# State-space mixer of a hybrid block: per-group VectorE products merged, and a subtraction moved to ScalarE biases

## The chip, the cores and the metric

One core of one Trainium2 chip runs the whole program. The metric is the device time of one execution in microseconds, the median of several runs; a profile is taken of one more execution.

## The reference

Two layers over 1024 latent tokens and 256 context tokens, width 1024. Each layer projects the normed tokens into three groups of heads: attention, a bidirectional state-space mixer (SSD) and a long convolution (Hyena, here by trigonometric matrices). Their outputs are concatenated and projected, and an MLP follows. All of it is fp32. The change touches the state-space mixer alone. For each chunk of 128 tokens, with 6 heads in 2 groups of 3:

```python
cum = jnp.cumsum(dtc * a, axis=2)
seg = cum[:, :, :, None, :] - cum[:, :, None, :, :]
decay = jnp.where(tri, jnp.exp(jnp.where(tri, seg, 0.0)), 0.0)
scores = jnp.einsum('bcihn,bcjhn->bcijh', cc, bc) * decay
y_diag = jnp.einsum('bcijh,bcjhp->bcihp', scores * dtc[:, :, None, :, :], xc)
y_off = jnp.einsum('bcihn,bchpn->bcihp', cc, prev) * jnp.exp(cum)[..., None]
```

This is done once forward and once backward in time. B and C (`bc`, `cc`) are shared by the 3 heads of a group.

## The kernel before

The program goes through each layer in three stages: the input projections with their convolutions (`stage_a`), the three mixers beside each other (`stage_b`), then the output projection and the MLP (`out_proj`, `mlp`). Products with weights are done as three fp32r matmuls on split high and low parts (L177, L178, L180; L191 to L193).

`stage_b` merges generators: attention (48 query tiles: scores L191 to L193, row maximum on VectorE L935, exponential on ScalarE L936, reciprocal L937, its spreading by matmul L941 and copy L943, transposes L952 that are copied out by L957 on ScalarE and L955 on VectorE, product with the values L964, L965), the state-space chunks (`ssm`), the convolution's filters and spectra (L1145 to L1181) and in layer 0 the modulation's columns (L307 to L315). The merge sets only the order in which the program is written. The tile framework then schedules: by its own model of the engines' times it decides the order of the instructions on every engine, and each engine runs its own queue strictly in that order, waiting on semaphores. So a change of a few instructions can reorder others that it doesn't touch.

Inside `ssm`, the function `scores(c)` prepares chunk c, for both directions at once. It loads the column sums as rows, broadcast over the partitions (`crow`, 12 x 128; its halves are Q and E, forward and backward), B (`bd`), C (`cd`) and the values (`xb`). A matmul gives B times C per group (L664), VectorE masks it with the two triangles into `gm` (L666), ScalarE takes exponentials of the sums into CE (L668, L669). VectorE subtracts the backward sums of each token from E (L670, one operation of 128 x 768) and takes the smaller of that and the forward difference, head by head (L672, six of 128 x 128); ScalarE takes the exponential (L673). VectorE then forms the masked scores Q and E from it (L678: 2 directions x 2 groups, 128 x 384 each), the values times the step sizes (L681), and the decayed queries CE times C (L683: 2 groups). `outputs(c)` multiplies (L693), adds the skip (L695), gates (L696) and squares (L697); `scaled(c)` finishes the norm (L704 to L715). There are 10 chunks in layer 0, from about 440 to 655 us, and 8 in layer 1, from about 2440 to 2615 us. `crow` alternates between two buffers, CE too. In layer 0, after the mixers, `out_proj` loads the mixers' outputs back (L974) and splits them (L160, L162); beside it the modulation of layer 1 loads its weights (L348) through one buffer that VectorE reads (L353, L355).

Of the kernel before, what the change touches and what calls it, by code (L numbers as in the profile page):

```python
# [12 lines left out]
AF = mybir.ActivationFunctionType  # L13
# [30 lines left out]
def V(t, off, shape):  # L44

    n = int(np.prod(shape))
    v = t[:, off:off + n]
    if len(shape) == 1:
        return v
    if len(shape) == 2:  # L50
        return v.rearrange("p (a b) -> p a b", a=shape[0])
    if len(shape) == 3:
        return v.rearrange("p (a b c) -> p a b c", a=shape[0], b=shape[1])
    return v.rearrange("p (a b c d) -> p a b c d", a=shape[0], b=shape[1], c=shape[2])
# [56 lines left out]
class K:  # L111
# [441 lines left out]
    def ssm(self, i):  # L553
        nc = self.nc
        sub, mul, add = ALU.subtract, ALU.mult, ALU.add
        st0, st1, st2, la, lb = (self.t(s) for s in ("H8", "U2", "H11", "H9", "H10"))
        P = lambda c: V(st0, 384 * c, [384]) if c < 6 else V(st1, 384 * (c - 6), [384]) if c < 9 else V(st2, 0, [384])
        dt, cum, dec, wl = (V(st2, 384 + 120 * j, [10, 12]) for j in range(4))
        spt = V(lb, 1536, [6, 10, 12])

        x = spt[:, 0]
        nc.vector.tensor_tensor(x, self.dtr, self.row(i, "dtb").unsqueeze(1).to_broadcast([128, 10, 12]), op=add)
        e = spt[:, 1]
# [8 lines left out]
        q = spt[:, 4]  # L572
# [9 lines left out]
        p = self.gs()  # L582
# [27 lines left out]
        for c in (8, 9, 0, 7, 1, 6, 2, 5, 3, 4):  # L610
            xb = xbr([4, 128])
            nc.sync.dma_start(xb, self.xbcD[:, 0:4, col(c):col(c) + 128])
            g = self.gs()
# [9 lines left out]
            g = self.gs()  # L623
# [8 lines left out]
        for q, order in enumerate(((8, 9, 0, 1, 2, 3, 4, 5, 6), (9, 8, 7, 6, 5, 4, 3, 2, 1))):  # L632
            r = slice(64 * q, 64 * q + 64)
            for c in order:
                t = tmr([384])[r, :]
                e = nc.vector
                e.tensor_tensor(z3(t), z3(P(c)[r, :]), dec[r, c, 6 * q:6 * q + 6].unsqueeze(2).to_broadcast([64, 6, 64]), op=mul)
                d = P(to(q, c))[r, :]
                e.tensor_tensor(d, d, t, op=add)
        yield 10  # L640

        tc_, yst = self.t("C2"), self.t("U0")
        ld1, ld2 = VRing((la, 0), (lb, 0)), VRing((tc_, 0), (tc_, 640))
        cer, ysr, xfr = VRing((st2, 864), (st2, 1632)), VRing((yst, 0), (yst, 384)), VRing((yst, 768), (tc_, 2176))
        gm, sq = V(tc_, 1280, [2, 2, 128]), V(tc_, 1792, [3, 128])

        def scores(c, done):
            ld, ldx = ld1([20, 128]), ld2([5, 128])
            crow, xz, bd, cd, xb = ld[:, 0:12], ld[:, 12:18], ld[0:64, 18:20], ldx[:, 0:2], ldx[:, 2:5].rearrange("p a b -> p (a b)")
            cols = slice(col(c), col(c) + 128)  # L650
            bc = lambda k: self.xbcD[:, k, cols].rearrange("(g p) t -> p g t", g=2)
            nc.sync.dma_start(bd, bc(0))
            nc.sync.dma_start(cd[0:64], bc(7))
            nc.sync.dma_start(crow, self.cumD[c:c + 1].to_broadcast([128, 12, 128]))
            nc.sync.dma_start(cd[64:128], bc(7))
            nc.sync.dma_start(xz, self.xbcD[:, 1:7, cols])
            nc.sync.dma_start(xb, self.xtD[c][:, 0:384])
            CE = cer([6, 128])
            Q, E = crow[:, 0:6], crow[:, 6:12]
            g = self.gs()  # L660
            if done:
                rms(g)
            for gr in range(2):
                nc.tensor.matmul(g[:, 128 * gr:128 * gr + 128], bd[:, gr, :], cd[0:64, gr, :], start=True, stop=True)  # L664
            R = root(g) if done else None
            nc.vector.tensor_tensor(gm, g[:, 0:256].rearrange("p (a b) -> p a b", a=2).unsqueeze(1).to_broadcast([128, 2, 2, 128]),  # L666
                                    self.tri.unsqueeze(2).to_broadcast([128, 2, 2, 128]), op=mul)
            nc.scalar.activation(CE[0:64], crow[0:64, 0:6], AF.Exp)  # L668
            nc.scalar.activation(CE[64:128], crow[64:128, 6:12], AF.Exp)  # L669
            nc.vector.tensor_tensor(E, E, cum[:, c, 6:12].unsqueeze(2).to_broadcast([128, 6, 128]), op=sub)  # L670
            for h in range(6):
                nc.vector.scalar_tensor_tensor(E[:, h, :], Q[:, h, :], cum[:, c, h:h + 1], E[:, h, :], op0=sub, op1=ALU.min)  # L672
            nc.scalar.activation(E, E, AF.Exp)  # L673

            for gr in range(2):
                h = slice(3 * gr, 3 * gr + 3)
                for q, (x, e) in enumerate(((Q, nc.vector), (E, nc.vector))):
                    e.tensor_tensor(x[:, h], E[:, h], gm[:, q, gr:gr + 1, :].to_broadcast([128, 3, 128]), op=mul)  # L678
            xf = xfr([384])
            for q, x in enumerate((xf, xb)):  # L680
                nc.vector.tensor_tensor(z3(x), z3(xb), dt[:, c, 6 * q:6 * q + 6].unsqueeze(2).to_broadcast([128, 6, 64]), op=mul)  # L681
            for gr in range(2):
                nc.vector.tensor_tensor(CE[:, 3 * gr:3 * gr + 3, :], CE[:, 3 * gr:3 * gr + 3, :],  # L683
                                        cd[:, gr, :].unsqueeze(1).to_broadcast([128, 3, 128]), op=mul)
            return R, (c, xz, ((xf, Q), (xb, E), (P(c), CE)))

        def outputs(c, xz, terms):
# [12 lines left out]
        def rms(p):  # L700

            for t in range(3):
                for b in range(4):
                    nc.tensor.matmul(p[32 * b:32 * b + 32, 256:288], self.ssel[:, t, :], sq[:, t, 32 * b:32 * b + 32], start=t == 0, stop=t == 2)  # L704

        def root(p):
            return self.rsq(None, p[:, 256:288], 32, 1.0 / 192)
# [8 lines left out]

        order = list(range(8)) + ([8, 9] if i == 0 else [])
        (_, cur), done = scores(order[0], None), None
        for n in range(len(order)):
            R, nxt = scores(order[n + 1], done) if n + 1 < len(order) else (None, None)  # L720
            if done and R is None:
                g = self.gs()
                rms(g)
                R = root(g)
            out = outputs(*cur)
            if done:
                scaled(*done, R)
            cur, done = nxt, out
            yield 12
        g = self.gs()  # L730
# [1057 lines left out]
```

## Time and profile before

| | us |
|---|---|
| median of 3 runs (lowest, highest) | 3657.69 (3657.3, 3661.86) |
| the profiled execution | 3666.86 |
| its span, first to last instruction | 3665.1 |
| TensorE busy | 3398.1 (93%) |
| VectorE busy | 1957.7 (53%) |
| ScalarE busy | 1255.7 (34%) |

The busy times are sums over the span, and stages differ: the three engines are read per stretch below. TensorE's end times are modelled, so its busy share is not its peak rate.

### The profile page before, as it was taken

Reading aid. Unit: us, or ns where it says so; the run is one execution under the profiler, and the core shown is the slowest. Engines: PE = TensorE matmul, PEld = TensorE weight load, DVE = VectorE, ACT = ScalarE, POOL = GpSimd, SP = SyncE. Lnnn points to the kernel's source line nnn. Section 1 sums busy time; section 2 is a strip of 40 time slices with the busy share of each in tenths; the row PEclk is TensorE's granted clock in tenths of the full one; section 3 lists DMA queues with packets and bytes.
Section 4 is the critical chain, followed back from the end, with each engine's and each line's share of the span. In section 5 each row is a group of like instructions: output and inputs, shape, how many; then the busy total and the mean of one; then the engine's idle time right before and its main releaser. Section 6 shows DMA issues by size and latency. Waiting matters only on the chain.

```text
span 3665.1 us, 51139 instructions
## 1 busy us (share of the span) xinstructions
PE 3398.1 (93%) x20636; PEld 2785.1 (76%) x20636; DVE 1957.7 (53%) x3172; ACT 1255.7 (34%) x2078; POOL 710.7 (19%) x479
## 2 busy tenths in 40 slices
PE   6899888888888999999999989988998999999999
PEld 3788767667767777888888777867787778888887
DVE  6576688667654766423323367679875332222223
ACT  4565444443332211111111256555434322111111
POOL 1000000011131322232322200000011433333332
PEclk9899989999999999999999999999999999999999
DMA  7345767587741223111111224577476311111112
GB/s 252 118 123 165 190 179 221 160 237 219 269 145 47 103 98 104 52 35 41 40 35 41 72 78 138 150 205 216 140 220 202 92 46 46 47 51 47 46 47 74
DMA packets 263042, 439.24 MB, mean 120 GB/s; under 512 B 33316, under 2 KB 172341, under 8 KB 256790
## 3 DMA queue, kind: packets, MB, share of 16 engines
q1 hardware_dynamic: 231654, 333.86, 29.3%
q0 software_dynamic: 31152, 102.12, 9.8%
q8 instruction: 162, 2.65, 0.3%
q14 instruction: 74, 0.61, 0.1%
HBM read 355.43 MB, written 80.47 MB: 119 GB/s over the span
## 4 chain that ended last, share of the span: by engine, by line
PE 68%; DMA 11%; DVE 10%; issue 7%; ACT 2%; POOL 1%; SPq 0%; POOLq 0%; DVEq 0%; ACTq 0%
PE psum L177 16%; PE psum L180 16%; PE psum L178 16%; PE psum L191 4%; PE psum L192 4%; PE psum L193 4%; DVE D L355 3%; DMA U<-in_wmod_dram 3%; PE psum L964 2%; PE psum L952 1%; DMA H<-cumD 1%; DMA H<-kD 1%; DVE st L935 1%; DMA Wp<-in_t_odd_dram 1%; PE psum L833 1%
## 5 line engine op out<-in xcount | busy, mean ns | idle before, releaser
L177 PE MATMUL psum<-H,Wp 128*128 128x512 f32 (+1 forms) x2112 | 788.5, 374 | 19.0 <-ACT H L160 12.6
L178 PE MATMUL psum<-H,Wp 128*128 128x512 f32 (+1 forms) x2112 | 786.7, 373 | 6.8 <-POOL H L162 5.8
L180 PE MATMUL psum<-H,Wp 128*128 128x512 f32 (+1 forms) x2112 | 679.0, 373 | 2.0 <-POOL Wp L162 1.8
L988 DVE SCALAR_TENSOR_TENSOR H<-psum,mod,H 128x1024 f32<-128x1024 f32 (+2 forms) x440 | 409.4, 955 | 463.0 <-PE psum L180 435.7
L162 POOL TENSOR_TENSOR Wp<-Wr,Wp 128x1024 fp32r<-128x1024 f32 x158 | 403.3, 2553 | 1204.8 <-ACT Wp L160 1185.9
L177 PEld LDWEIGHTS psum<-H,Wp 128*128 128x128 f32 x2112 | 399.0, 189 | 94.5 <-ACT H L160 13.1
L178 PEld LDWEIGHTS psum<-H,Wp 128*128 128x128 f32 x2112 | 398.9, 189 | 78.6 <-POOL H L162 7.3
L160 ACT CAST Wp<-Wr 128x1024 fp32r<-128x1024 f32 (+1 forms) x210 | 216.1, 1029 | 707.5 <-PE psum L180 639.3
L177 PE MATMUL psum<-C,Wp 128*128 128x512 f32 (+1 forms) x1200 | 448.8, 374 | 6.9 <-DVE H L988 6.0
L180 PEld LDWEIGHTS psum<-H,Wp 128*128 128x128 f32 x2112 | 397.4, 189 | 75.7 <-issue 4.6
L178 PE MATMUL psum<-C,Wp 128*128 128x512 f32 (+1 forms) x1200 | 447.3, 373 | 0.0
L1007 DVE TENSOR_TENSOR U<-U 128x1280 f32<-128x1280 f32 (+1 forms) x64 | 90.4, 1415 | 592.0 <-ACT U L1006 318.3
L180 PE MATMUL psum<-C,Wp 128*128 128x512 f32 (+1 forms) x1200 | 369.7, 373 | 0.0
L177 PEld LDWEIGHTS psum<-C,Wp 128*128 128x128 f32 x1200 | 226.2, 189 | 59.3 <-DVE H L988 12.1
L180 PEld LDWEIGHTS psum<-C,Wp 128*128 128x128 f32 x1200 | 226.2, 188 | 43.9
L178 PEld LDWEIGHTS psum<-C,Wp 128*128 128x128 f32 x1200 | 226.5, 189 | 42.3
L1006 ACT ACTIVATE U<-psum 128x1024 f32<-128x1024 f32 x64 | 65.6, 1026 | 515.6 <-PE psum L180 510.8
L355 DVE SCALAR_TENSOR_TENSOR D<-U,cpad,D 128x1024 f32<-128x1024 f32 x84 | 144.5, 1758 | 84.5 <-DMA U<-in_wmod_dram 84.4
L162 POOL TENSOR_TENSOR C<-U,C 128x1280 fp32r<-128x1280 f32 (+1 forms) x64 | 173.6, 2713 | 69.2 <-ACT C L160 69.2
L936 ACT ACTIVATE H<-psum,st 128x1280 f32<-128x1280 f32 x96 | 127.6, 1329 | 133.3 <-DVE st L935 130.4
L191 PE MATMUL psum<-H,H 96*128 96x512 f32 (+3 forms) x356 | 143.9, 404 | 21.0 <-ACT C L957 7.1
L191 PE MATMUL psum<-H,Wp 128*128 128x256 f32 (+1 forms) x464 | 144.5, 314 | 18.4 <-ACT H L403 7.0
(410 smaller groups left out, 5494.6 us busy)
## 6 DMA issues: line engine op xcount, KB each, us to landing
Wr<-in_wff_dram SPq DMA_DIRECT2D x128, 512.0 KB, 3.5
Wp<-in_t_odd_dram POOLq DMA_DIRECT2D x32, 1024.0 KB, 7.0
U<-in_wmod_dram SPq DMA_DIRECT2D x48, 512.0 KB, 3.2
C<-in_wmod_dram SPq DMA_DIRECT2D x32, 512.0 KB, 5.5
Wr<-in_wout_dram SPq DMA_DIRECT2D x32, 512.0 KB, 3.6
Wr<-in_win_dram SPq DMA_DIRECT2D x28, 512.0 KB, 3.3
H<-cumD SPq DMA_DIRECT2D x18, 768.0 KB, 4.8
kD<-H SPq DMA_DIRECT2D x40, 288.0 KB, 3.2
```

Source lines behind the costliest of these rows:

```text
L160: nc.scalar.copy(h, src)
L162: e.tensor_tensor(l, src, h.bitcast(F32), op=ALU.subtract)
L177: mm(out, lh, rh, start=first, stop=False)
L178: mm(out, lh, rl, start=False, stop=False)
L180: mm(out, ll, rh, start=False, stop=last)
L191: mm(out, lh, rh, start=first, stop=False)
L192: mm(out, lh, rl, start=False, stop=False)
L193: mm(out, ll, rh, start=False, stop=last)
L355: nc.vector.scalar_tensor_tensor(acc[:, s], w, c, acc[:, s], op0=ALU.mult, op1=ALU.add)
L936: nc.scalar.activation(E[:, hh], p, AF.Exp, bias=st[:, 1, hh:hh + 1], accum_out=st[:, 0, hh:hh + 1])
L988: self.nc.vector.scalar_tensor_tensor(x, p(a, b - a), self.mod[i][:, row, st:st + 1], x, op0=ALU.mult, op1=ALU.add)
L1007: nc.vector.tensor_tensor(r, r, r, op=ALU.mult)
```

## The change

Three edits, all in `ssm`. The four products that make the masked scores become two of 128 x 768, with the mask of each group broadcast over its three heads by a four-dimensional view; the two products of the decayed queries become one of 128 x 768. The subtraction of the backward sums leaves VectorE: ScalarE adds the negated sums as a per-partition bias, head by head, six operations of 128 x 128 (line 673 after the change). The negated sums are made once per layer by a VectorE operation of 128 x 60 (line 642), in free columns of an existing tile.

```diff
--- before.py
+++ after.py
@@ -638,6 +638,8 @@
                 d = P(to(q, c))[r, :]
                 e.tensor_tensor(d, d, t, op=add)
         yield 10
+        ncb = V(st2, 2400, [10, 6])
+        nc.vector.tensor_scalar(ncb, cum[:, :, 6:12], -1.0, None, op0=mul)
 
         tc_, yst = self.t("C2"), self.t("U0")
         ld1, ld2 = VRing((la, 0), (lb, 0)), VRing((tc_, 0), (tc_, 640))
@@ -667,21 +669,19 @@
                                     self.tri.unsqueeze(2).to_broadcast([128, 2, 2, 128]), op=mul)
             nc.scalar.activation(CE[0:64], crow[0:64, 0:6], AF.Exp)
             nc.scalar.activation(CE[64:128], crow[64:128, 6:12], AF.Exp)
-            nc.vector.tensor_tensor(E, E, cum[:, c, 6:12].unsqueeze(2).to_broadcast([128, 6, 128]), op=sub)
+            for h in range(6):
+                nc.scalar.activation(E[:, h, :], E[:, h, :], AF.Identity, bias=ncb[:, c, h:h + 1])
             for h in range(6):
                 nc.vector.scalar_tensor_tensor(E[:, h, :], Q[:, h, :], cum[:, c, h:h + 1], E[:, h, :], op0=sub, op1=ALU.min)
             nc.scalar.activation(E, E, AF.Exp)
 
-            for gr in range(2):
-                h = slice(3 * gr, 3 * gr + 3)
-                for q, (x, e) in enumerate(((Q, nc.vector), (E, nc.vector))):
-                    e.tensor_tensor(x[:, h], E[:, h], gm[:, q, gr:gr + 1, :].to_broadcast([128, 3, 128]), op=mul)
+            two = lambda x: x.rearrange("p (g h) t -> p g h t", g=2)
+            for q, x in enumerate((Q, E)):
+                nc.vector.tensor_tensor(two(x), two(E), gm[:, q].unsqueeze(2).to_broadcast([128, 2, 3, 128]), op=mul)
             xf = xfr([384])
             for q, x in enumerate((xf, xb)):
                 nc.vector.tensor_tensor(z3(x), z3(xb), dt[:, c, 6 * q:6 * q + 6].unsqueeze(2).to_broadcast([128, 6, 64]), op=mul)
-            for gr in range(2):
-                nc.vector.tensor_tensor(CE[:, 3 * gr:3 * gr + 3, :], CE[:, 3 * gr:3 * gr + 3, :],
-                                        cd[:, gr, :].unsqueeze(1).to_broadcast([128, 3, 128]), op=mul)
+            nc.vector.tensor_tensor(two(CE), two(CE), cd.unsqueeze(2).to_broadcast([128, 2, 3, 128]), op=mul)
             return R, (c, xz, ((xf, Q), (xb, E), (P(c), CE)))
 
         def outputs(c, xz, terms):
```

The scheduler's answer to it, at three places. In the rows after the change, lines behind 640 count differently: L670 and L671 are the exponentials before L668 and L669, L673 the new biases, L675 the head-by-head minimum (before L672), L676 the exponential (before L673), L680 and L684 the merged products, L683 the values (before L681).

ScalarE, chunk 5 of layer 1. H_900 is `crow`, H_898 holds CE and the sums, H_926 and C_927 are attention's exponentials and their transposes. Before:

```order
L668 ACTIVATE H_898_17390<-H_900_17392 64x768
L669 ACTIVATE H_898_17390<-H_900_17392 64x768
L936 ACTIVATE H_926_18062,st_19977<-psum,st_19977 128x1280
L957 COPY C_927_18063<-psum 128x512
L204 ACTIVATE rqy_18836<-rqa_18834 128x32
L957 COPY C_927_18063<-psum 128x512
L207 ACTIVATE rqy_18836<-rqy_18836 128x32
L673 ACTIVATE H_900_17392<-H_900_17392 128x768
L936 ACTIVATE H_926_18062,st_19977<-psum,st_19977 128x1280
```

After:

```order
L670 ACTIVATE H_898_17411<-H_900_17413 64x768
L671 ACTIVATE H_898_17411<-H_900_17413 64x768
L936 ACTIVATE H_926_18088,st_20015<-psum,st_20015 128x1280
L673 ACTIVATE H_900_17413<-H_900_17413,H_898_17411 128x128 x6
L204 ACTIVATE rqy_18868<-rqa_18866 128x32
L957 COPY C_927_18089<-psum 128x512 x2
L936 ACTIVATE H_926_18088,st_20015<-psum,st_20015 128x1280
L207 ACTIVATE rqy_18868<-rqy_18868 128x32
L676 ACTIVATE H_900_17413<-H_900_17413 128x768
```

The six biases stand behind the tile's first L936 and ahead of the copies L957 and the second L936.

VectorE, the same chunk (`st` and `att` are attention's). Before:

```order
L670 TENSOR_TENSOR H_900_17392<-H_900_17392,H_898_17390 128x768
L683 TENSOR_TENSOR H_898_17390<-H_898_17390,C_923_17982 128x384 x2
L681 TENSOR_TENSOR C_923_17982<-C_923_17982,H_898_17390 128x384
L672 SCALAR_TENSOR_TENSOR H_900_17392<-H_900_17392,H_898_17390 128x128
L200 TENSOR_SCALAR rqa_18834<-psum 128x32
L666 TENSOR_TENSOR C_923_17982<-psum,kc 128x512
L672 SCALAR_TENSOR_TENSOR H_900_17392<-H_900_17392,H_898_17390 128x128 x5
L935 TENSOR_REDUCE st_19977<-psum 128x1
L965 TENSOR_TENSOR att_19791<-psum,att_19791 128x128
L209 TENSOR_TENSOR rqa_18834<-rqa_18834,rqy_18836 128x32
L678 TENSOR_TENSOR H_900_17392<-H_900_17392,C_923_17982 128x384 x2
L695 SCALAR_TENSOR_TENSOR U_924_17983<-H_899_17391,pk_77,psum 128x128 x3
```

After:

```order
L935 TENSOR_REDUCE st_20015<-psum 128x1
L965 TENSOR_TENSOR att_19829<-psum,att_19829 128x128
L675 SCALAR_TENSOR_TENSOR H_900_17413<-H_900_17413,H_898_17411 128x128 x6
L695 SCALAR_TENSOR_TENSOR U_924_18005<-H_899_17412,pk_77,psum 128x128 x3
L937 RECIPROCAL st_20015<-st_20015 128x2
L209 TENSOR_TENSOR rqa_18866<-rqa_18866,rqy_18868 128x32
L696 TENSOR_TENSOR U_924_18005<-U_924_18005,H_899_17412 128x384
L210 SCALAR_TENSOR_TENSOR rqa_18866<-rqa_18866,rqy_18868 128x32
L680 TENSOR_TENSOR H_900_17413<-H_900_17413,C_923_18004 128x768
L215 SCALAR_TENSOR_TENSOR r_90<-rqa_18866,rqy_18868 32x32 x4
L955 COPY C_927_18089<-psum 128x512
L680 TENSOR_TENSOR H_900_17413<-H_900_17413,C_923_18004 128x768
```

The subtraction is gone, attention's second row maximum (L935) stands ahead of the six minima instead of behind them, and each merged product stands where two were.

SP's queue at the end of layer 0's mixers. C_520, C_521, C_519 and C_542 are the mixers' outputs being loaded for `out_proj`; U_577 is the modulation weights' one buffer, `att` for attention's last results being stored. Before:

```order
L974 DMA C_520_8758<-mixD 128x2x512
L348 DMA U_577_9957<-in_wmod_dram 128x1024
L966 DMA mixD<-att_8612 128x128
L974 DMA C_521_8762<-mixD 128x2x512
L348 DMA U_577_9957<-in_wmod_dram 128x1024
L974 DMA C_542_9096<-mixD 128x2x768
L974 DMA C_519_8754<-mixD 128x2x512
L348 DMA U_577_9957<-in_wmod_dram 128x1024
L966 DMA mixD<-att_8687 128x128
```

After:

```order
L348 DMA U_577_9978<-in_wmod_dram 128x1024
L974 DMA C_520_8779<-mixD 128x2x512
L348 DMA U_577_9978<-in_wmod_dram 128x1024 x2
L966 DMA mixD<-att_8530 128x128
L974 DMA C_521_8783<-mixD 128x2x512
L348 DMA U_577_9978<-in_wmod_dram 128x1024
L966 DMA mixD<-att_8633 128x128
L974 DMA C_542_9117<-mixD 128x2x768
L348 DMA U_577_9978<-in_wmod_dram 128x1024 x2
L966 DMA mixD<-att_8708 128x128
L974 DMA C_519_8775<-mixD 128x2x512
```

Before, the load into C_519 (the buffer that attention's transposes held) stood ahead of the store of the last attention tile, with two weight loads ahead of it; after, it stands behind that store and behind six weight loads.

## Rows read from the trace of the kernel before

**Rows 1.** Busy time by engine, both state-space stretches: start:end, length, then engines, clock.

```profile
440.00:655.00 215.00, 173.87 (x1704) 139.17 (x1703) 175.63 (x422) 103.84 (x203) 13.10 (x22) 0.87 0.76 206
2440.00:2615.00 175.00, 153.28 (x1526) 124.26 (x1525) 153.85 (x350) 99.24 (x180) 9.38 (x15) 0.97 0.58 166
```

**Rows 2.** Busy time by engine in 50 us pieces, columns as above.

```profile
500.00:550.00 50.00, 42.89 (x448) 37.03 (x440) 47.33 (x104) 25.53 (x50) 2.90 (x5) 0.93 0.57 167
550.00:600.00 50.00, 42.10 (x471) 35.56 (x471) 40.42 (x103) 27.32 (x53) 3.83 (x8) 0.93 0.94 274
600.00:650.00 50.00, 42.05 (x481) 33.91 (x479) 36.21 (x101) 22.65 (x44) 2.07 (x3) 0.90 0.63 171
2450.00:2500.00 50.00, 41.10 (x329) 31.64 (x328) 47.70 (x86) 27.74 (x44) 1.30 (x2) 0.97 0.33 104
2500.00:2550.00 50.00, 46.78 (x512) 40.98 (x511) 45.66 (x119) 33.84 (x67) 4.49 (x8) 1.00 0.83 249
2550.00:2600.00 50.00, 41.31 (x439) 32.35 (x437) 39.53 (x97) 24.18 (x43) 2.84 (x4) 0.93 0.71 180
```

**Rows 3.** VectorE groups by form, whole span: count | busy us, mean ns | idle before.

```profile
L678 DVE TENSOR_TENSOR H<-H,C 128x384 f32<-128x384 f32 x72 | 37.0, 548 | 0.2
L683 DVE TENSOR_TENSOR H<-H,C 128x384 f32<-128x384 f32 x36 | 18.4, 550 | 2.7 <-DMA C<-xbcD 2.6
L670 DVE TENSOR_TENSOR H<-H,H 128x768 f32<-128x768 f32 x18 | 17.2, 953 | 8.9 <-ACT H L669 8.9
```

**Rows 4.** VectorE in order of time, layer 0, one chunk: start us, us.

```profile
556.84 0.95 DVE L670 TENSOR_TENSOR H<-H,H 128x768 f32<-128x768 f32 x1
557.71 1.02 DVE L683 TENSOR_TENSOR H<-H,C 128x384 f32<-128x384 f32 x2
```

**Rows 5.** ScalarE groups by form, whole span, columns as in rows 3.

```profile
L837 ACT ACTIVATE H<-psum,pk 96x384 fp32r<-96x384 f32 x40 | 22.4, 578 | 13.3 <-PE psum L833 12.5 <-DMA qD<-H 0.4
L495 ACT ACTIVATE H<-psum,pk 128x128 fp32r<-128x128 f32 x32 | 11.6, 362 | 33.3 <-PE psum L486 27.3 <-DVE H L496 5.8
L943 ACT COPY att<-psum 128x128 f32<-128x128 f32 x48 | 13.0, 270 | 38.6 <-PE psum L941 38.4
```

**Rows 6.** ScalarE in order of time, layer 0: two such operations back to back.

```profile
221.06 1.06 ACT L837 ACTIVATE H<-psum,pk 96x384 fp32r<-96x384 f32 x2
```

**Rows 7.** What TensorE waited for, 430 to 660 us: us in total, times, longest.

```profile
PE psum L964 <- DVE mod L315: 6.9, 3, 5.5
PE psum L952 <- ACT H L936: 1.8, 3, 1.2
```

**Rows 8.** What TensorE waited for, 2430 to 2625 us.

```profile
PE psum L952 <- ACT H L936: 8.8, 7, 3.5
PE psum L191 <- ACT C L957: 3.5, 6, 1.8
PE psum L941 <- DVE st L937: 3.5, 1, 3.5
PE psum L693 <- DVE C L666: 2.2, 2, 1.4
PE psum L191 <- ACT H L936: 2.0, 1, 2.0
```

**Rows 9.** What ScalarE waited for, 430 to 660 us, then 2430 to 2625 us.

```profile
ACT H L936 <- DVE st L935: 16.4, 9, 3.0
...
ACT H L936 <- DVE st L935: 20.6, 12, 3.7
```

**Rows 10.** SP's queue in order of time, end of layer 0's mixers.

```profile
1018.01 0.88 SPq L974 DMA_DIRECT2D C<-mixD  x2
1020.83 0.38 SPq L966 DMA_DIRECT2D mixD<-att  x1
```

**Rows 11.** TensorE in order of time at the same place: [idle before <- what ended it].

```profile
1024.78 1.22 PE L177 MATMUL psum<-H,Wp 128*128 128x512 f32 x2 [7.67 <-ACT H L160]
...
1030.63 0.79 PE L178 MATMUL psum<-H,Wp 128*128 128x512 f32 x1 [4.63 <-POOL H L162]
```

## The prediction

> **What bounds the kernel now.** The change touches only the state-space chunks, so I first read the busy times of the two stretches in which they run [rows 1]. In layer 0 (215 us) TensorE is busy 173.87 us, VectorE 175.63 and ScalarE 103.84; in layer 1 (175 us) 153.28, 153.85 and 99.24. The reader should see two things. TensorE's work isn't touched, so whatever is won must come out of its idle time: 215 - 173.87 = 41.1 us and 175 - 153.28 = 21.7 us, together 62.8 us. And no engine is full throughout: VectorE is (47 of 50 us) in two of the six 50 us pieces, while in the others it is at 36 to 46 [rows 2].
>
> [...]
>
> Next I read what TensorE waited for. In layer 0 I count 6.9 us for VectorE and 1.8 for attention's exponential on ScalarE [rows 7] (others, each under 3 us, are left out); in layer 1 3.5 + 2.2 = 5.7 us for VectorE and 8.8 + 3.5 + 2.0 = 14.3 for ScalarE [rows 8]. Together VectorE ends 12.6 us of TensorE's 62.8 and ScalarE 16.1. But 1.8 + 8.8 + 2.0 = 12.6 of ScalarE's part is attention's exponential L936, and that operation itself sat waiting 16.4 + 20.6 = 37.0 us for VectorE's row maximum [rows 9]. Passing those 12.6 us on, VectorE stands behind 25.2 us, which is 40% of TensorE's idle time, and ScalarE ends 16.1 us, 26%. The two overlap; I use both as weights for extra or missing work on each queue. That is a choice, and the softest step of this sum.
>
> **The change part by part.** *VectorE loses work, 18 chunks.* An operation of 128 x 768 takes 953 ns alone, one of 128 x 384 takes 548 to 550 [rows 3], but in a queue they overlap: the next operation starts 0.87 us after L670, and two of 384 take 1.02 us where one takes 0.55, so the second adds 0.47 [rows 4]. Per chunk the subtraction gives back 0.87; four masked products become two, 4 x 0.47 - 2 x 0.87 = 0.14; two products of CE become one, 2 x 0.47 - 0.87 = 0.07. Sum 1.08 us, in 18 chunks 19.5 us. From the durations alone it would be 0.953 + (4 x 0.548 - 2 x 0.953) + (2 x 0.550 - 0.953) = 1.39 us, or 24.9 us. I take 19.5, since VectorE's queue is mostly full here, and keep 24.9 as the other end.
>
> [...]
>
> The merged products' four-dimensional view might cost something, which the rows above don't show; nothing on the other side excludes a loss of one more overlap of 0.08 us each, 3 x 18 x 0.08 = 4.3 us, which I leave to the range. The negated sums are one VectorE operation per layer on 60 columns, ahead of the chunks; it is less than one operation of 384, 0.55 us, and two of them stay inside 1.1 us. I count nothing: VectorE has idle time ahead of the chunks, and if it hasn't, the cost is 1.1 us.
>
> *ScalarE gains work.* The six biased operations of 128 x 128 have no row. Nearest is L495, the same size with a per-partition scale, 362 ns; a plain copy of that size is 270 [rows 5]. Two of L837 take 1.06 us where one takes 0.578, so the second overlaps by about 0.10 [rows 5, 6]. So six take 6 x 0.362 - 5 x 0.10 = 1.67 us. The ends are 6 x 0.17 + 0.10 = 1.1 and 6 x 0.362 = 2.2 us. I take 1.67, from the row that also has a per-partition operand. In 18 chunks 30.1 us, on an engine that is busy 52% of these stretches. What is queued behind the six matters: in the new order 13 of the 18 groups of six have one of attention's own operations (the exponential L936 or the copies L957 and L943) within the next two rows, as in the ScalarE piece shown above; these are what TensorE waits for. 13 x 1.67 = 21.7 us.
>
> *The chain inside a chunk.* The minimum now waits for ScalarE instead of the subtraction. From the end of L669, 0.95 us and six minima gave way to six biases with the minima trailing by one. That is about equal, and the next chunk's loads have two buffers; I count nothing. VectorE used to wait for L669 at the subtraction, 8.9 us in all [rows 3]; that wait moves to the first minimum and isn't won.
>
> *On the path.* VectorE's relief by its weight: 19.5 x 0.40 = -7.8 us. ScalarE's delay by its weight: 21.7 x 0.26 = +5.6 us.
>
> *What the scheduler moves.* At the end of layer 0's mixers, SP's queue now has the load into C_519 behind the last attention tile's store. Before, that load was issued at 1018.01 us and the store at 1020.83 [rows 10], so it comes at least 2.8 us later, and TensorE, which sat idle 7.67 and then 4.63 us there for the splitting of just such loads [rows 11], waits with it: +2.8 us. The ends are 0 (other loads are later still) and 12.3 (those two waits once more, for the weight loads that now stand ahead). In the rest of both stages hundreds of instructions change neighbours with no sign that I can name. How much that can do, I take from how TensorE's busy time varies over six pieces of the same work [rows 2]: their mean is 42.7 and the deviations have a spread of 2.1 us; the mixers fill some 18 such pieces in both layers, so a reshuffle is worth 2.1 x 4.2 = 9 us either way.
>
> **Sum:** -7.8 + 5.6 + 2.8 = +0.6 us. The profiled execution took 3666.86 us, so its like would take 3667.5. That execution stands 9.2 us above the median of the runs, so I set the change against the median: 3657.69 + 0.6, about 3658 us. No change that can be measured; by that I mean within 0.2%, 7.3 us, about what a measurement of this kernel can tell from none.
>
> **The rivals.** *First: VectorE decides, faster.* For it: its queue is full in two of the pieces [rows 2], and attention's exponentials wait 37.0 us for it [rows 9]. Against: in layer 0 TensorE's named waits on it are few [rows 7]. Then the whole 19.5 us shows, ScalarE's work fits its idle half, and with +2.8 the time is 3657.69 - 16.7 = 3641 us.
>
> *Second: ScalarE's queue decides, slower.* Attention's chain goes from the row maximum over L936, the transposes and L957 back to TensorE, and each of these steps can stand behind six biases. The wait that goes from VectorE is replaced by one for ScalarE. For it: in layer 1 ScalarE already ends 14.3 us of TensorE's waits [rows 8]. Against: it is idle for almost half of the stretch [rows 1], so the six may fall into that. If in all 13 groups attention's operation is ready when the six start, the cost is 21.7 us in full, against VectorE's -7.8 and with +2.8: 3657.69 + 16.7 = 3674 us. It decides from the point where 8 of the 13 are so (8 x 1.67 = 13.4, with -7.8 and +2.8 a loss of 8.4 us).
>
> *Third: the order alone.* The two costs cancel and the new neighbours decide: 3658 with 9 us on either side, 3649 to 3667. This is the forecast's own range.
>
> *Fourth: the merge does not save.* If the four-dimensional views cost what they save, VectorE loses only the subtraction, 18 x 0.87 = 15.7 us instead of 19.5; by the weight 0.40 that is 1.5 us less, 3659.5, so it can't be told from the forecast by time.
>
> **How the numbers follow.** The forecast with its spread of 9 us, the third and the fourth rival with it, gets 0.63: of that 0.11 lies below -7.3 us, 0.15 above +7.3, and 0.37 between. The first rival gets 0.22: 0.18 faster and 0.04 within 0.2%, where another order gives some of it back. The second gets 0.15: 0.11 slower and 0.04 within. Sums: faster 0.29, within 0.2% 0.45, slower 0.26. More than half lies outside the middle, so the forecast's own range, 3649 to 3667, stands beside the full one: 3642 reaches to just short of the first rival's time, 3674 to the second's, and a tenth is left out on each side.
>
> **What would show it.** Right: L670's 17.2 us gone from VectorE, the products L678 and L683 at 54 operations of about 0.95 us, VectorE's busy time in these stretches some 20 us down, ScalarE's some 30 us up in 108 operations near 0.36 us, and TensorE's idle time there still about 60 us, with less of it ended by VectorE. The first rival: that idle time down by 15 us or more. The second: waits of TensorE for L936 and L957 up from 16.1 us to 30 or more, and those operations starting straight behind a bias. The prediction is wrong in its mechanism if TensorE's idle time changes elsewhere, in stretches without a state-space chunk, by more than in these two, or if the six biases take less than 1.1 or more than 2.2 us.

## The result, and the profile after

The changed kernel takes 3678.72 us (median of 5 runs, 3673.04 to 3687.77), against 3657.3 us for the kernel before (5 runs). The ratio is 1.0054, with a 95% interval of 1.004 to 1.0068: about 21 us slower, and 4.7 us above the upper end of the predicted range. Two executions that lie far above all others (3866.22 us of the kernel before, 5824.98 us of x6) are left out of every comparison below.

The profiled execution of the changed kernel took 3675.48 us (span 3673.3). That of before stood 9.6 us above this median, so the two profiles lie only 8.6 us apart. They show how things changed better than how much.

The instructions came out as priced. The page's first part for the changed kernel, the busy time of both stretches (compare [rows 1]), and single lines of its code with min/median/max in ns:

```profile
PE 3402.6 (93%) x20636; PEld 2789.2 (76%) x20636; DVE 1937.5 (53%) x3102; ACT 1286.3 (35%) x2186; POOL 712.8 (19%) x479
```

```profile
440.00:655.00 215.00, 174.98 (x1746) 140.41 (x1746) 171.13 (x399) 123.07 (x270) 12.90 (x22) 0.90 0.80 218
2440.00:2615.00 175.00, 152.03 (x1449) 123.63 (x1449) 142.37 (x309) 108.71 (x222) 9.42 (x15) 0.93 0.59 168
```

```profile
L680 DVE TENSOR_TENSOR H<-H,C x36: 942/951/960, 468.2 to 2602.9; 128x768 f32<-128x768 f32 x36
L684 DVE TENSOR_TENSOR H<-H,C x18: 948/952/959, 466.9 to 2592.9; 128x768 f32<-128x768 f32 x18
L673 ACT ACTIVATE H<-H,H x108: 384/387/424, 441.1 to 2596.4; 128x128 f32<-128x128 f32 x108
```

VectorE lost 1957.7 - 1937.5 = 20.2 us (19.5 predicted), ScalarE gained 1286.3 - 1255.7 = 30.6 us (30.1 predicted). TensorE's idle time in the two stretches is 40.0 + 23.0 = 63.0 us, as before (62.8). And yet the kernel is slower. What TensorE waited for after the change, 430 to 660 us (compare [rows 7]), 660 to 1035 us, and 2430 to 2625 us (compare [rows 8]):

```profile
PE psum L191 <- DMA H<-qD: 13.6, 2, 12.4
PE psum L952 <- ACT H L936: 11.2, 7, 3.6
...
PE psum L177 <- ACT H L160: 11.0, 1, 11.0
PE psum L952 <- ACT H L936: 8.0, 6, 3.5
...
PE psum L952 <- ACT H L936: 7.0, 7, 3.3
PE psum L191 <- ACT C L957: 5.2, 7, 1.9
PE psum L941 <- DVE st L937: 4.3, 1, 4.3
```

Lines of the same kind from the kernel before, 430 to 660 us and 660 to 1035 us:

```profile
PE psum L547 <- DVE U L533: 7.8, 1, 7.8
PE psum L191 <- DMA H<-qD: 4.1, 1, 4.1
...
PE psum L952 <- ACT H L936: 13.7, 10, 5.8
PE psum L177 <- ACT H L160: 7.7, 1, 7.7
```

From 430 to 660 us the wait for attention's exponential L936 rose from 1.8 to 11.2 us. It is tempting to read the six biases into that: L936 runs on the engine that got the new work. The experiments show that this reading is wrong. Behind 660 us the same wait fell from 13.7 to 8.0, so over both windows it rose from 15.5 to 19.2 us. And before's longest wait between 430 and 660 us, 7.8 us for VectorE's L533, is not among the changed kernel's.

### The profile page after: what moved, and what is told of

It is laid out like the page before. It is cut to its first block, busy times and chain, and to the rows that moved or that the text cites. A ratio compares the mean times of both kernels' runs of the same rounds, so it can differ in the third digit from the quotient of the medians.

```text
span 3673.3 us, 51155 instructions
## 1 busy us (share of the span) xinstructions
PE 3402.6 (93%) x20636; PEld 2789.2 (76%) x20636; DVE 1937.5 (53%) x3102; ACT 1286.3 (35%) x2186; POOL 712.8 (19%) x479
## 4 chain that ended last, share of the span: by engine, by line
PE 70%; DVE 10%; DMA 10%; issue 6%; ACT 2%; POOL 1%; SPq 0%; POOLq 0%; DVEq 0%; ACTq 0%
PE psum L177 17%; PE psum L180 17%; PE psum L178 17%; PE psum L191 4%; PE psum L192 4%; PE psum L193 4%; DVE D L355 3%; DMA U<-in_wmod_dram 3%; PE psum L964 2%; PE psum L952 1%; DMA H<-cumD 1%; DMA C<-specD 1%; DVE st L935 1%; PE psum L693 1%; DMA Wp<-in_t_odd_dram 1%
## 5 line engine op out<-in xcount | busy, mean ns | idle before, releaser
L988 DVE SCALAR_TENSOR_TENSOR H<-psum,mod,H 128x1024 f32<-128x1024 f32 (+2 forms) x440 | 409.8, 956 | 485.8 <-PE psum L180 457.1
L936 ACT ACTIVATE H<-psum,st 128x1280 f32<-128x1280 f32 x96 | 127.6, 1329 | 121.0 <-DVE st L935 120.8
L952 PE MATMUL psum<-ident,H 128*128 128x128 f32 x960 | 135.4, 289 | 31.3 <-ACT H L936 30.5
```

What stands on the lines that cost most here:

```text
L936: nc.scalar.activation(E[:, hh], p, AF.Exp, bias=st[:, 1, hh:hh + 1], accum_out=st[:, 0, hh:hh + 1])
L952: nc.tensor.transpose(self.ps[:, 128 * k:128 * k + 128], e[:, 128 * k:128 * k + 128], self.ident)
L988: self.nc.vector.scalar_tensor_tensor(x, p(a, b - a), self.mod[i][:, row, st:st + 1], x, op0=ALU.mult, op1=ALU.add)
```

## The experiments

**How kernels with a fixed order are made.** The scheduler gives a new order to each kernel that it sees. To part an edit's own cost from the order that comes with it, some kernels below hold every engine to a given sequence:

```diff
         body(tc, aps, out)
+        _pin(tc, nc)
```

`_pin` chains each engine's instructions, in the sequence of a table, by dependencies that order and don't signal. "Old order" is that of before, "new order" that of the changed kernel. Instructions that one kernel has and the other lacks stand at the places that the expectations name. The kernel before with `_pin` and its own order was not timed, so a cost of `_pin` itself is not shown by a run of its own; x5 and x17, with `_pin` and 0.9989 and 0.9995, leave little room for one.

All were timed against before on the same chip. The last three columns are differences of means from before in us. The middle one is time x (1 - granted clock) averaged over the runs. In short pieces of before's trace that clock is 1.00 (424 to 430 us, 2533.6 to 2536) or 0.50 (456 to 459); L192's matmul of 96x512 is followed by the next after 0.23 us at 1.00 (from 2534.01) and after 0.43 at 0.50 (from 458.65). So the column is an estimate of what the lower level takes away, as if TensorE worked through it at half its pace. The last is what remains, idle time. From the scatter of the runs, the three differences are uncertain by 2 to 7 us each (95%), so only the larger ones in the last two columns can be read one by one. (By the same sum, an estimate too, TensorE's work at full clock is 3398.1 - 0.035 x 3665.1 = 3269.8 us in the profile before and 3402.6 - 0.036 x 3673.3 = 3270.4 after: the same.) The changed kernel itself has a mean clock of 0.9628 over its 5 runs against 0.9654 in 114 runs of before: 136.9 - 126.8 = 10 us, of 18 between the means of the same runs (3679.8 and 3661.9).

| | ratio to before, 95% interval | all | clock | idle |
|---|---|---|---|---|
| x1 edits, old order | 1.0033 [1.0018, 1.0047] | +11.7 | +7.7 | +4.1 |
| x2 no edits, new order | 1.0069 [1.0049, 1.0089] | +26.7 | +4.2 | +22.4 |
| x3 biases, own order | 1.008 [1.0062, 1.0098] | +30.7 | +6.8 | +23.9 |
| x4 merges, own order | 1.005 [1.0031, 1.007] | +20.1 | +5.8 | +14.3 |
| x5 merges, old order | 0.9989 [0.9977, 1.0] | -4.4 | -1.6 | -2.7 |
| x6 biases, old order | 1.003 [1.0018, 1.0043] | +12.7 | +8.7 | +4.0 |
| x7 null edit, own order | 1.0054 [1.0037, 1.0071] | +20.1 | +9.6 | +10.5 |
| x8 exponentials moved, own order | 1.0017 [1.0002, 1.0032] | +5.0 | +7.2 | -2.2 |
| x9 no edits, new order in layer 0 | 1.0037 [1.0024, 1.005] | +14.8 | -2.1 | +16.9 |
| x10 no edits, new order in layer 1 | 1.0035 [1.0021, 1.005] | +12.2 | +13.2 | -1.0 |
| x11 as x1, biases late | 1.0009 [0.9994, 1.0024] | +3.3 | +2.1 | +1.2 |
| x12 merges, subtraction on GpSimd | 1.0007 [0.9995, 1.002] | +4.3 | +6.8 | -2.5 |
| x13 as x5, attention first | 1.0019 [1.0009, 1.0029] | +6.2 | +2.6 | +3.6 |
| x14 as x10, attention first | 1.0072 [1.006, 1.0084] | +26.4 | +22.7 | +3.7 |
| x15 changed, attention first | 1.0073 [1.0061, 1.0085] | +26.5 | +11.7 | +14.8 |
| x16 as x11, attention first | 0.9995 [0.9986, 1.0004] | -1.1 | -0.4 | -0.8 |
| x17 as x5, once more | 0.9995 [0.9981, 1.0009] | -2.3 | -3.0 | +0.7 |

### Cost or order: x1 to x4

x1 has all three edits and the old order.

> The changed kernel's instructions in the order of the kernel before on every engine: the six biases stand right behind the second exponential of the decayed queries, the merged products where the first (queries' half) or the last (keys' half, decayed queries) of the separate ones stood. So it pays and earns what the edits cost, with no new neighbours. Delay theory (ScalarE's six biases, 1.85 us in a row, hold up attention's exponential and copies, and that outweighs VectorE's 20 us): slower than before by 10 us or more, 3667 to 3680, with TensorE's waits for L936 and L957 up in both layers' chunk stretches. Order theory (the 21 us come from the scheduler's new order): 3645 to 3662, no more than 5 us above before. First rival of the prediction (VectorE decides): 3637 to 3645.

x2 has no edit and the new order.

> The kernel before's own instructions in the order that the changed kernel has on every engine: the subtraction stands on VectorE directly ahead of the first minimum, the separate products where the merged ones stood. New neighbours, none of the edits' costs. Order theory: most of the loss is there, 3670 to 3685, since nothing of VectorE's relief comes with it. Delay theory: within 5 us of before, 3652 to 3662.

x3 and x4 have one half of the diff each, and the scheduler's own order.

> Only the subtraction becomes six biases on ScalarE, the products stay apart; the scheduler orders as it likes. Delay theory: as slow as the whole change or slower by the 4 us of the merges, 3675 to 3685. Order theory: a third order of its own, so anywhere from 3645 to 3685, and its distance from before says nothing of the biases.

> Only the products are merged, the subtraction stays on VectorE; the scheduler orders as it likes. Worth 18 x 0.21 = 3.8 us of VectorE's time. Delay theory: 3652 to 3660, a little faster than before or the same. Order theory: a fourth order, anywhere from 3645 to 3685; a time over 3667 could only come from the order, because no instruction got longer and ScalarE got nothing.

The new order costs 0.69% with none of the edits, as much as the whole change or more (the intervals overlap). The edits cost 0.33% in the old order. The two don't add up (1.0054 for both): in the new order the same edits cost nothing that shows. x4 is the clearest miss of the delay theory: ScalarE gets nothing there, VectorE has 4 us less to do, and 20 us are lost. Both theories are true in part, the order in the larger one.

### The edits one at a time in the old order: x5, x6, x17

> Only the products are merged, and every engine keeps the order of the kernel before. VectorE has 54 instructions less and some 4 us less to do, nothing else changes. If the loss of x4_merges_only (20 us) is its new order: within 4 us of before or a little faster, 3654 to 3664 against before's 3661. If the four-dimensional view itself costs something that the durations don't show: over 3668.

> x5_merges_old_order once more, the same kernel. If the merges are worth VectorE's 3.8 us: 2 to 6 us faster than before, 0.9985 to 0.9995. If x5 was chance: 0.9995 to 1.001. Either way some 20 us faster than the changed kernel, with a granted clock near before's 0.965 and TensorE's idle time near 264 us.

> Only the subtraction becomes six biases, and every engine keeps the order of the kernel before, with the six right behind the second exponential of the decayed queries. If the 10 to 12 us of x1_cost_alone are the biases' on ScalarE's queue: 3670 to 3680. If they are the merged products', or a clock that was lower by chance: 3658 to 3666.

The merges win 2 to 4 us, about VectorE's 3.8, though x5's interval ends at 1.0 and x17's goes beyond it, and x17's 0.9995 lies on the border of its two expectations. VectorE's busy time fell from 1957.7 to 1953.3 us. That is what the overlapping rows gave [rows 4]. The durations alone [rows 3] would have given 18 x (4 x 0.548 - 2 x 0.953 + 2 x 0.550 - 0.953) = 7.8 us, an estimate; but these operations overlap in the queue (two of 128 x 384 took 1.02 us, one alone 0.55). The biases cost 11 to 13 us, and the trace shows one place where. ScalarE in x6, layer 1 (its L960 is before's L957, its L670, L671 before's L668, L669):

```profile
2533.76 0.84 ACT L670 ACTIVATE H<-H 64x768 f32<-64x768 f32 x1 [2.43 <-DMA H<-cumD]
2534.62 0.84 ACT L671 ACTIVATE H<-H 64x768 f32<-64x768 f32 x1
2535.49 1.86 ACT L673 ACTIVATE H<-H,H 128x128 f32<-128x128 f32 x6
2537.26 0.56 ACT L960 COPY C<-psum 128x512 f32<-128x512 f32 x1
```

The first of these rows in the kernel before:

```profile
2531.31 0.84 ACT L668 ACTIVATE H<-H 64x768 f32<-64x768 f32 x1 [1.62 <-DMA H<-cumD]
```

TensorE in x6 behind it, then the same matmul in the kernel before:

```profile
2537.88 0.80 PE L191 MATMUL psum<-H,H 96*128 96x512 f32 x1 [4.40 <-ACT C L960]
```

```profile
2533.66 0.50 PE L191 MATMUL psum<-H,H 96*128 96x512 f32 x1 [1.85 <-ACT C L957]
```

The queue stands still for a chunk's rows (2.43 us, 1.62 before), then runs two exponentials and six biases, with attention's copy behind them. TensorE's wait grows from 1.85 to 4.40 us: the six are 1.8 of that, and the longer standstill 0.8. The matmul that ends it takes 0.80 instead of 0.50 us, and in the table 8.7 of the 12.7 us are clock. This is the prediction's second rival at work.

### A null edit: x7, x8

x7 only swaps two lines:

```diff
-            nc.scalar.activation(CE[0:64], crow[0:64, 0:6], AF.Exp)
             nc.scalar.activation(CE[64:128], crow[64:128, 6:12], AF.Exp)
+            nc.scalar.activation(CE[0:64], crow[0:64, 0:6], AF.Exp)
```

> The kernel before with the two exponentials of the decayed queries written in the other order: the same instructions, the same number, the same durations; the scheduler then gives some 1300 of TensorE's 18079 instructions, 365 of VectorE's and 170 of ScalarE's another place, about as many as in the changed kernel. Order theory, in the form that the old order is an uncommonly good one and nearly any other is worse: 3670 to 3690, with nothing computed otherwise. In the form that orders scatter about a mean: as likely faster as slower, 3645 to 3680. Delay theory: 3661, the same.

> A second one of the kind: both exponentials of the decayed queries written behind the large exponential of the scores. Same instructions, another order (some 1640 of TensorE's, 475 of VectorE's, 215 of ScalarE's moved). Order theory: 3670 to 3690 if the old order is uncommonly good, 3645 to 3680 if orders scatter. Delay theory: 3655 to 3665.

In x8 both lines stand behind `nc.scalar.activation(E, E, AF.Exp)`, so the backward decayed queries are taken from sums that the subtraction has overwritten; its instructions are the same.

Nothing is computed otherwise in x7, and it is 20 us slower. With x2, x8 and, with half of the edits each, x3 and x4, that makes five other orders, all slower than the old one, by 5 to 31 us (x3 has the biases' cost in it, and x8's interval begins at 1.0002). By these five the old order is an uncommonly good one, and what the changed kernel lost first is that order.

### Where the order costs: x9, x10

> The kernel before's instructions in the changed kernel's order up to layer 0's MLP, and in their own order from there on. x2_order_alone lost 25 us with the new order in both layers; outside the mixers the two orders are the same. Order theory with the loss where most instructions moved (layer 0 has ten of the eighteen chunks): 15 to 25 us slower than before. If the loss is in layer 1: within 5 us of before.

> The other half: the old order in layer 0, the changed kernel's order in layer 1's mixers. The two halves should add up to the 25 us of x2_order_alone, if layers don't act on each other: 3665 to 3675 if this half costs 5 to 10 us.

The halves add up: 0.37% + 0.35% against 0.69%. In layer 0 the order costs idle time (16.9 us), in layer 1 clock (13.2 us). x9 has none of the biases; what TensorE waited for in it, 430 to 660 us and 660 to 1035 us:

```profile
PE psum L191 <- DMA H<-qD: 12.9, 1, 12.9
PE psum L952 <- ACT H L936: 9.9, 5, 4.4
...
PE psum L177 <- ACT H L160: 11.2, 1, 11.2
```

These are the changed kernel's waits (13.6, 11.2, 11.0) without a single bias. x10, which has the old order in layer 0, has 1.2 us for L936 and 3.2 for qD from 430 to 660 us, like before. So the rise of L936's wait there, which looked like the biases' doing, is the order's, and so is the longer wait for a transfer of the convolution.

In layer 1 the order costs through the clock. The stretch of [rows 1] and what TensorE waited for in x10, 2430 to 2625 us:

```profile
2440.00:2615.00 175.00, 153.42 (x1430) 124.71 (x1430) 145.31 (x332) 91.01 (x164) 8.62 (x14) 0.89 0.56 157
...
PE psum L952 <- ACT H L936: 7.5, 5, 2.9
PE psum L941 <- DVE st L937: 3.8, 1, 3.8
PE psum L191 <- ACT C L957: 3.7, 7, 1.3
```

In sum these waits are no longer than before's [rows 8], but the granted clock is 0.89 against 0.97 (0.93 in x9, which has before's order there). ScalarE ahead of the longest wait for L936:

```profile
2551.44 0.84 ACT L668 ACTIVATE H<-H 64x768 f32<-64x768 f32 x1 [5.72 <-DMA H<-cumD]
2552.30 0.84 ACT L669 ACTIVATE H<-H 64x768 f32<-64x768 f32 x1
2553.16 1.33 ACT L936 ACTIVATE H<-psum,st 128x1280 f32<-128x1280 f32 x1
```

The chunk's matmuls that follow, in x10 and in before (min/median/max ns):

```profile
L693 PE MATMUL psum<-H,H x12: 417/418/418, 2556.2 to 2559.0; 128*64 128x128 f32 x12
```

```profile
L693 PE MATMUL psum<-H,H x12: 272/272/273, 2559.9 to 2561.4; 128*64 128x128 f32 x12
```

And two pieces of 5 us later, in x10 (columns as in [rows 1]):

```profile
2561.00:2566.00 5.00, 1.35 (x13) 1.11 (x11) 0.85 (x4) 0.00 (x0) 0.00 (x0) 1.00 1.25 272
2566.00:2571.00 5.00, 3.87 (x15) 3.09 (x16) 4.35 (x16) 3.33 (x6) 0.00 (x0) 0.53 0.68 206
```

After a wait of 2.88 us the same matmul takes 418 instead of 272 ns; after 3.79 us without work (the wait for L937) the next piece runs at 0.53, which is nearly all at 0.50. These two waits are paid twice, as idle time and as slow matmuls behind them. Not every wait is: behind before's 1.85 us, shown above, the matmul took 0.50 us, where x6's took 0.80 behind 4.40. What decides between the two is not shown.

### Later biases, another engine: x11, x12

x11 moves the six behind what stood behind them, for example (ScalarE, layer 1):

```diff
-L673 ACTIVATE (six biases)
 L957 COPY C<-psum
+L673 ACTIVATE (six biases)
```

> The changed kernel's instructions in the old order, as x1_cost_alone, but in 10 of 18 chunks the six biases stand behind the next one to ten operations of ScalarE's queue (attention's exponentials and copies among them), as far as the first minimum had time to wait in the trace of x6_biases_old_order. Nothing else moves. Delay theory (the six cost what stands behind them on ScalarE): most of x1's 12 us go, 3655 to 3667 against before's 3661 to 3664. If the cost lies elsewhere (the clock, the minima's wait, accesses to memory): 3668 to 3680 as x1. If the minima are late now and hold up VectorE's queue: over 3680.

x12 keeps the subtraction as one operation, on another engine:

```diff
-            nc.vector.tensor_tensor(E, E, cum[:, c, 6:12]...
+            nc.gpsimd.tensor_tensor(E, E, cum[:, c, 6:12]...
```

> Merged products and the subtraction on GpSimd, in the old order of the other engines. VectorE is relieved of the same 20 us as in the change, and ScalarE gets nothing. GpSimd is busy 13 of 215 us in layer 0's chunk stretch and takes 2.5 us for a product of 128 x 1024, so about 1.9 us for this one, twice what VectorE takes. Delay theory: 3648 to 3658, faster than both kernels, because the relief stays and the delay goes. If VectorE's relief is worth little: 3658 to 3664. If GpSimd's work makes VectorE's operations longer, or the minima wait for it: over 3665.

x11 takes back 8.4 of x1's 11.7 us with the same instructions: most of the biases' cost in the old order is what they hold up. x12 misses: with GpSimd's help before isn't beaten. VectorE's busy time is 1948.3 us there, only 5.0 under x5's 1953.3, although it has 18 operations of 0.95 us less; one group in x12 and in x5, 430 to 660 us:

```profile
L680 DVE TENSOR_TENSOR C<-C,H 128x384 f32<-128x384 f32 x15 | 11.2, 747 | 2.1 <-DMA C<-xtD 2.0
```

```profile
L680 DVE TENSOR_TENSOR C<-C,H 128x384 f32<-128x384 f32 x15 | 8.2, 550 | 1.2 <-DMA C<-xtD 1.1
```

The same product takes 747 instead of 550 ns on average: four of the 15 take 1.05 to 1.83 us, and each of the four started while GpSimd's subtraction ran (1.46 to 2.67 us each). They may be long because of it; how is not shown.

### Attention ahead of the waiting exponential: x13 to x16

In each, ready operations of attention move ahead of the chunk's exponentials on ScalarE, for example (x14):

```diff
+L936 ACTIVATE H,st<-psum,st
 L668 ACTIVATE H<-H
 L669 ACTIVATE H<-H
-L936 ACTIVATE H,st<-psum,st
```

> x5_merges_old_order with one to four of attention's ready operations (exponentials and copies) moved ahead of the chunk's exponentials on ScalarE in 10 of 18 chunks, nothing else. Head-of-queue theory (attention's operations stand behind a waiting exponential, TensorE waits for them and its clock falls): 3 to 10 us faster than x5, so 3645 to 3657 against before's 3661. If the chunk's own chain is what counts there (it now starts 0.5 to 2 us later): 3660 or more, no gain over x5.

> x10_order_layer1 with the same kind of move, in both layers, by its own trace. Its layer 1 lost 12 us, and TensorE's waits for attention's exponential there (2.88 and 2.55 us) follow waits of ScalarE of 5.72 and 1.67 us for a DMA. Head-of-queue theory: 6 to 14 us faster than x10, 3658 to 3668. If the order costs elsewhere: 3670 to 3676, as x10.

> The changed kernel in its own order with attention's ready operations moved ahead of the chunk's exponentials, and so ahead of the six biases too, in 10 of 18 chunks. Head-of-queue theory: 6 to 14 us faster than the changed kernel, 3664 to 3673. If its loss has another cause: 3675 to 3682.

> x11_biases_late (all three edits, old order, biases late) with the same kind of move in 10 of 18 chunks. Head-of-queue theory: 3 to 10 us faster than x11, 3653 to 3660. Against x13, which keeps the subtraction on VectorE, it shows what VectorE's relief is worth once ScalarE's queue holds nobody up: nothing if it is slower than or equal to x13, as much as my weight of 0.40 said (6 us for 15.7) if it is that much faster.

The theory falls: x13 and x14 are 9 to 14 us slower than what they start from, x15 is 4 us slower than the changed kernel and x16 4 us faster than x11 (both within the intervals). What TensorE waited for in x14, 2525 to 2630 us:

```profile
PE psum L704 <- DVE U L714: 4.7, 1, 4.7
PE psum L693 <- DVE C L666: 3.6, 1, 3.6
PE psum L941 <- DVE st L937: 3.4, 1, 3.4
PE psum L952 <- ACT H L936: 2.6, 1, 2.6
```

L936's wait did fall, from 6.0 us in x10 in the same window. In its place TensorE waits 8.3 us for the chunk's own masks L666 and outputs L714. So here the chunk's chain is as near to the edge as attention's, and moving one ahead holds up the other. Whether that is all of x14's loss isn't shown, since the move was made in layer 0 too. Why the same move doesn't hurt in x16 stays open.

## Why the prediction was wrong

**The step that failed: "so a reshuffle is worth 2.1 x 4.2 = 9 us either way".** I took the order as neutral, with a spread worked out from six pieces of one and the same order. x2 puts it at 27 us on its own, in both layers alike, and x7 shows 20 us from two swapped lines. So the term of the order, 2.8 +- 9 us in the sum, measured 27 us for the changed kernel's order, and not one of the five other orders came out faster than the old one. That an order better than its neighbours is likely to get worse could not be read from the rows I had; it took x2 and x7.

**The order's one named term, +2.8 us: right in size, by luck.** The first `out_proj` wait grew from 7.67 [rows 11] to 10.97 us, as forecast, but the second shrank by as much, from 4.63 [rows 11] to 1.22. The loss at this place is a third wait, for VectorE's L988, that the sum didn't name. TensorE after the change, then the matmul of the third row in the kernel before:

```profile
1024.06 1.22 PE L177 MATMUL psum<-H,Wp 128*128 128x512 f32 x2 [10.97 <-ACT H L160]
1026.50 0.79 PE L178 MATMUL psum<-H,Wp 128*128 128x512 f32 x1 [1.22 <-POOL H L162]
...
1040.19 0.47 PE L177 MATMUL psum<-H,Wp 128*128 128x512 f32 x1 [3.67 <-DVE H L988]
```

```profile
1041.12 0.47 PE L177 MATMUL psum<-H,Wp 128*128 128x512 f32 x1 [0.76 <-DVE H L988]
```

From the end of attention's last matmul (the start of the first wait) to this one it is 24.0 us before and 27.1 after.

**A reading that was wrong.** I left out layer 0's other waits as "each under 3 us". Two of them are longer: 7.8 us for VectorE's L533, shown above, and 4.1 for the transfer qD. With the 7.8 VectorE's weight would have been 33.0 / 62.8 = 0.53 in place of 0.40, and the forecast 2.5 us faster, further from the result.

**ScalarE's term, +5.6 us: right mechanism, half the size in the old order.** The six take 1.85 us (1.67 forecast). They cost 11 to 13 us in the old order (x6, and x1 with the merges' gain in it); all three edits with the biases late stand at 3 us (x11). My weight of 0.26 came from idle time alone; some 8 of the 12 us are clock, for which the sum had no term at all. In the new order no run times the biases alone; there all three edits together cost nothing that shows (x2 against the changed kernel).

**VectorE's term, -7.8 us: open.** The merges' 3.8 us came out at -2 to -4. For the subtraction's 15.7 us, by the weight 0.40 worth 6.3, the runs disagree. By the comparison that x16's expectation names, x16 against x13, its leaving VectorE wins 7 us (0.9995 against 1.0019, intervals apart), as the weight said. But x17, with it on VectorE and no move of attention's operations, stands at 0.9995 too, so the 7 us may be what that move costs in x13. So it isn't shown that VectorE's other work stood before TensorE while attention's exponential waited 37 us for the row maximum [rows 9], nor that it didn't.

**The rivals.** The first is dead: VectorE lost 20 us and the kernel became slower. The second's time, 3674, lies near the result, but its mark, over 30 us of TensorE's waits on L936 and L957, was not reached (11.2 + 1.3 and 7.0 + 5.2 = 24.7), and most of the rise there is the order's (x9). The third had the right cause, but left the sign open and was too narrow. The fourth is not needed: VectorE's busy time fell by what was worked out for the merges.

In the profile pair the sum could not be told: 8.6 us, of which the clock (0.965 to 0.964) and idle time (267.0 to 270.7) take about half each. Of the 3.7 us of idle time only 0.2 lie in the two stretches with chunks, so the prediction's own sign of a wrong mechanism, more change elsewhere than in these two, was there.

No version here is shown to beat the kernel before. The merges in the old order (x5, x17: 0.9989 and 0.9995) and x16 (0.9995) come nearest, 20 us or more faster than the changed kernel.

## What to carry to other kernels

Where a scheduler sets the order, an edit has two prices, its own (12 us here, x1) and that of the order which comes with it (27 us, x2); time the old instructions in the new order, or a null edit, before you explain a wait by the new work beside it. Work put on an engine that is idle half of its time can cost what stands behind it in that queue (8.4 of x1's 11.7 us went when the biases stood later, x11), so place it behind what others wait for. And price a wait of TensorE above its length: the matmuls after it can be slower (418 instead of 272 ns behind 2.88 us in x10). When one wait shrinks or grows, look whether the next one gives it back (here 4.63 to 1.22 us beside 7.67 to 10.97).

## What the runs showed of the hardware

The spread between runs of one kernel goes with the clock too: the fastest of 114 runs of before (3647.02 us) had a mean granted clock of 0.971, the slowest (3676.95 us) 0.963, and over all runs time and clock go against each other (correlation -0.76). A difference of 0.008 x 3660 = 29 us is just what lies between those two. I had read the clock in the profile and thought of it as given; it varies by itself from run to run, and the order moves it: by 13.2 us in x10 and 22.7 us in x14.
